# Padding four kinds of tiles to whole multiples of 128 bytes in a two-layer hybrid attention trunk

## The chip, the cores and the metric

One core of a Trainium2 chip runs the whole program, in one launch. The metric is the device time of an execution in microseconds, of which the median of several runs is taken; lower is better.

## The reference

Two layers over 256 tokens of width 1024, in float32. Each layer normalises x, multiplies it by one wide input matrix, runs four small attention branches (stick breaking, gated linear, gated delta rule, dilated) of four heads each on slices of the product, gates and merges them, projects the result, adds it to x, and then does the same with an MLP of width 4096 with a squared relu.

```python
def hybrid_layer(x, g_mix, g_mlp, w_in, ..., w_branch, w_out, w_mlp_in, w_mlp_out):
    h = rms_norm(x, g_mix)
    (sb_q, sb_k, sb_v, gla_q, ..., dil_v, gate_logits) = jnp.split(h @ w_in, IN_OFFSETS, axis=-1)
    o_sb = stick_breaking_attention(...)
    o_gla = gla_branch(...)
    o_dn = deltanet_branch(...)
    o_dil = dilated_branch(...)
    gates = jax.nn.sigmoid(gate_logits.reshape(B, S, N_BRANCH, D_MODEL))
    merged = jnp.zeros_like(x)
    for n, o in enumerate((o_sb, o_gla, o_dn, o_dil)):
        merged = merged + gates[:, :, n] * (o.reshape(B, S, BRANCH_WIDTH) @ w_branch[n])
    x = x + merged @ w_out
    h = rms_norm(x, g_mlp)
    return x + jnp.square(jax.nn.relu(h @ w_mlp_in)) @ w_mlp_out
```

## The kernel before

**The stream of weights.** All weights lie in HBM as a list of units of 128 x 2048 float32, in the order in which they are used. Half a unit (128 x 1024, 512 KB) is loaded at a time into a tile raw (six of them), and split into two parts of type float32r: whi by a cast on ACT (line 247), wlo as the rest on DVE (line 248), five buffers of each. Activations are split in the same way into a high and a low part. A product is then three passes of matmuls: high by high, high weights by low activations, low weights by high activations.

**The dense matmuls.** All go through the helper mm (line 198 and 199), mm(out, stationary, moving). Each loads 128 x 128 weights and moves 256 columns, 1024 bytes in each partition. Half a unit makes 24 of them.

- Input products, gates and the first MLP product (unit_F, mmF, line 398): weights whi or wlo stationary, activations ah or al (8 x 256 columns) moving, one PSUM bank with the tag bg at a time. Three of the input products go token by token (unit_T, line 417), with ah or al stationary and whi or wlo moving.
- Branch products (unit_br, line 1246): whi or wlo stationary, oh or ol moving, in banks bg.
- Output projection and second MLP product (units_out, line 447): whi or wlo stationary, and mh or ml (output projection) or uh or ul (MLP, 32 x 256 columns each) moving, summed over all units in four banks fa and fb, eight sums at once.
- The small product "mini" (unit_mini, line 431): whi stationary with 64 columns instead of 128, ah or al moving.

**The small work.** The four branches run as threads of generators that take one step after each half of a unit (small, line 1139), with matmuls of their own in float32 (line 199 too) and transposes against the identity at the beginning of the tile C.

**Where tiles lie.** Pools are laid out one behind another in each partition: cons (C, MK, x, PR, NR), wp (raw, whi, wlo), acts (ah, al), sm (small tiles, among them nea), and then the pool of a stage: for the mixing (d6 three times, mg, s8, dlT0, ..., oh, ol), for the MLP (uh, ul, rl, sq). Each tile takes its bytes rounded up to a multiple of 32. C begins at byte 16512, a multiple of 128, and takes 5696 bytes (1422 columns); PR takes 3488 (2 x 433 columns); nea takes 32, twice; d6 takes 6240 (6 x 260 columns), three times. All others from C to ah are multiples of 128. From these sizes follow the offsets modulo 128: raw, whi, wlo, ah, al and NR at 96, the MLP's uh and ul at 32, and in the mixing mh, ml, oh, ol and the tiles of the branches at 64, d6 at 32, 96 or 0. The steps inside a tile (1024 bytes between slices of activations, 512 or more between those of weights) are multiples of 128.

Of the kernel before, what the change touches and what calls it, by code (L numbers as in the profile page):

```python
# [9 lines left out]
F32 = mybir.dt.float32  # L10
# [9 lines left out]
NL = 2  # L20
# [53 lines left out]
# columns of the packed parameters of a layer  # L74
P_GMIX, P_GMLP, P_CONV, P_DTB, P_ALOG, P_GLAB = 0, 8, 16, 40, 44, 48
P_GLAG, P_DNG, P_DILQ, P_DILK, P_LR2, NPAR = 49, 113, 177, 241, 305, 433
# columns of the constants
C_ID, C_NEGU, C_NEG1, C_UT, C_GT, C_STR, C_SBN, C_DIL = 0, 128, 256, 384, 512, 640, 768, 896
C_COS, C_SIN, C_SEL, C_S32, C_I32, C_H4, C_AB, NCON = 1280, 1312, 1344, 1346, 1378, 1410, 1414, 1422
LV = (1, 2, 4, 8, 16, 32, 64)  # L80

# [37 lines left out]
def lay_out(inp):  # L119
    a = {k: np.asarray(v) for k, v in inp.items()}  # L120
    w_in, w_br, w_out, w_mi, w_mo = (a[k] for k in ("w_in", "w_branch", "w_out", "w_mlp_in", "w_mlp_out"))
    W = np.zeros((len(UNITS), 128, 2048), np.float32)

    def kcols(w, c0, n=256):
        """[p][kt][column]"""
        return w[:, c0:c0 + n].reshape(8, 128, n).transpose(1, 0, 2).reshape(128, 8 * n)

    def fcols(w, c0):
        """[p][half of the columns][kt][column]"""
        return w[:, c0:c0 + 256].reshape(8, 128, 2, 128).transpose(1, 2, 0, 3).reshape(128, 2048)  # L130

    def krows(w, r0, halves=1):
        """[p][half of the columns][kt][column]"""
        n = 1024 // halves
        return w[r0:r0 + 256].reshape(2, 128, halves, n).transpose(1, 2, 0, 3).reshape(128, 2048)

    for n, (l, kind, arg) in enumerate(UNITS):
        if kind == "inF":
            W[n] = fcols(w_in[l], OFF[arg])
        elif kind == "inT":  # L140
            W[n] = kcols(w_in[l], OFF[arg])
        elif kind == "mini":
            m = np.zeros((1024, 32), np.float32)
            m[:, 0:8] = w_in[l][:, 2320:2328]
            m[:, 8:24] = w_in[l][:, 1280:1296]
            W[n][:, :256] = kcols(m, 0, 32)
        elif kind == "gate":
            W[n] = fcols(w_in[l], OFF["gates"] + arg[0] * 1024 + arg[1] * 256)
        elif kind == "br":
            W[n] = krows(w_br[l, arg], 0, 2)  # L150
        elif kind == "wo":
            W[n] = krows(w_out[l], arg * 256)
        elif kind == "mi":
            W[n] = fcols(w_mi[l], arg * 256)
        else:
            W[n] = krows(w_mo[l], arg * 256)
    P = np.zeros((NL, 128, NPAR), np.float32)
    for l in range(NL):
        P[l][:, P_GMIX:P_GMIX + 8] = a["norm_mix_g"][l].reshape(8, 128).T
        P[l][:, P_GMLP:P_GMLP + 8] = a["norm_mlp_g"][l].reshape(8, 128).T  # L160
        P[l][:, P_CONV:P_CONV + 24] = a["dn_conv_w"][l].reshape(6, 128, 4).transpose(1, 0, 2).reshape(128, 24)
        P[l][:, P_DTB:P_DTB + 4] = a["dn_dt_bias"][l][None]
        P[l][:, P_ALOG:P_ALOG + 4] = a["dn_a_log"][l][None]
        P[l][:, P_GLAB] = a["gla_b_lr"][l]
        P[l][:, P_GLAG:P_GLAG + 64] = a["gla_norm_g"][l][None]
        P[l][:, P_DNG:P_DNG + 64] = a["dn_norm_g"][l][None]
        P[l][:, P_DILQ:P_DILQ + 64] = a["dil_q_norm_g"][l][None]
        P[l][:, P_DILK:P_DILK + 64] = a["dil_k_norm_g"][l][None]
        for r in (8, 40):
            P[l][r:r + 16, P_LR2:P_LR2 + 128] = a["gla_w_lr2"][l]  # L170
    X = np.ascontiguousarray(a["x"].reshape(256, 8, 128).transpose(2, 1, 0).reshape(128, 2048))
    C, M = constants()
    return {"xin": X, "w": W, "par": P, "con": C, "msk": M}


@with_exitstack
def trunk(ctx: ExitStack, tc: tile.TileContext, xin, w, par, con, msk, out, dbg=None, nl=NL):
# [14 lines left out]
    def r3(ap, a):  # L192
        return ap.rearrange("p (a b) -> p a b", a=a)
# [10 lines left out]
    # ---------------- constants and x  # L204
    C = cons.tile([128, NCON], F32, name="C")
    MK = cons.tile([128, 5 * 128], U8, name="MK")
    x = cons.tile([128, 8, 256], F32, name="x")
    PR = cons.tile([128, NL, NPAR], F32, name="PR")
# [18 lines left out]
    # ---------------- the stream of weights  # L227
# [22 lines left out]
    def split_upto(h):  # L250
        """h counts halves of units"""
        while state["split"] <= min(h, 2 * total - 1):
            k = state["split"]
            hi = wp.tile([128, 1024], F32R, name="whi", bufs=HALVES)
            lo = wp.tile([128, 1024], F32R, name="wlo", bufs=HALVES)
            splits[k] = (hi, lo)
            src = raws.pop(k)
            if wcols(k // 2) == 256:
                # both parts side by side
                src, both = r3(src[:, :128], 4), r3(hi[:, :256], 4)  # L260
                ACT.copy(both[:, :, 0:32], src)
                DVE.tensor_sub(both[:, :, 32:64], src, both[:, :, 0:32].bitcast(F32))
            elif k == 0:
                state["first"] = (src, hi, lo)
            else:
                n = 512 if k == 1 else 1024
                for c in range(0, 1024, n):
                    split_part(src, hi, lo, slice(c, c + n))
            state["split"] += 1
            dma_upto(k + RAW)  # L270
# [15 lines left out]
    nc.sync.dma_start(C[:, C_NEG1 + 128:], con[:, C_NEG1 + 128:])  # L286
# [4 lines left out]
    # ---------------- small helpers  # L291
    def rsqrt(v, n, name):
        """v: [128, n] in SBUF, > 0"""
        y = sm.tile([128, n], F32, name=name + "y")
        t = sm.tile([128, n], F32, name=name + "t")
        first_guess(v, y, t)
        yield from pause(name)
        newton(v, y, t, POOL if NPOOL else None)
        return y

    def pause(name):
        """slack between a step and the one that reads it on another engine, in halves of units"""
        for _ in range(PAUSE[name]):
            yield
# [19 lines left out]
    class Norm:  # L324
        """x times the gain, feature-major and split; the root mean square is applied to what is made of it"""
# [28 lines left out]
        def rows(self):  # L354
            """1 / rms of each token, on every partition"""
# [9 lines left out]
        def scaled(self, t):  # L365
            """x over the root mean square"""
            self.t = t
            for kt in range(8):
                POOL.tensor_tensor(t[:, kt, :], x[:, kt, :], self.R, op=OP.mult)  # L369

        def flip(self):
            """from here on what is made of it needs no scale"""
# [12 lines left out]
    def half(h, evac_first=False):  # L385
        """weights of half h of the current unit; the halves after it are begun"""
# [11 lines left out]
    def mmF(o, wh, wl, c, h, kts=8, new=False):  # L398
        """feature-major product: three passes; that over the operand split last comes last"""
# [8 lines left out]
    def unit_F(h, new=False):  # L408
        """yields after each half, then a bank [128, 2, 256], feature-major; new: h has only just been made"""
# [7 lines left out]
    def unit_T(h):  # L417
        """token-major, a bank [128, 2, 256]"""
# [12 lines left out]
    def unit_mini(h):  # L431
        """feature-major [64, 256]: by the high parts of the weights and, 32 rows on, by the low ones"""
# [14 lines left out]
    def units_out(h, units, nm):  # L447
        """feature-major products in four banks [128, 2, 256], added to x; the last unit goes by output"""
# [49 lines left out]
    # ---------------- one layer  # L498
# [31 lines left out]
    def mixing(l, pr, mp, nm):  # L530
# [7 lines left out]

        def split_pair(ps):
# [4 lines left out]
        def to_feature(o, br, tag):  # L544
            """o: token-major [128, 2, 256] in SBUF -> split feature-major"""
# [7 lines left out]
        def head_rms(o, gs, br, tag, need=None):  # L553
            """o: [128, 2, 4, 64]; gs: silu of the gate times the gain"""
# [16 lines left out]
        # ---- gated delta rule: the gates and their decays  # L571
        def decay_chain():
            yield ("mini",)
            nea = sm.tile([128, 4], F32, name="nea")
# [24 lines left out]
            # rows and columns of the running sums of g  # L599
# [15 lines left out]
            got["E"] = E = T([6, 260], "d6", 3).rearrange("p a b -> p (a b)")[:, :1536].rearrange(  # L615
# [11 lines left out]
        # the products with the queries, and the values  # L627
# [33 lines left out]
        # ---- gated delta rule  # L661
        def dn_chain():
# [4 lines left out]
            pre = T([6, 260], "d6", 3)[:, :, :256]  # L667
# [38 lines left out]
            MT = T([6, 260], "d6", 3).rearrange("p a b -> p (a b)")[:, :1536].rearrange(  # L706
# [23 lines left out]
            # (I + M)^-1 transposed: blocks of 32 by substitution, all heads at once, then by doubling.  # L730
            # mc[j, (t, h), k]: the blocks of -M transposed
# [31 lines left out]
            def half_y(t, s):  # L763
                """levels 32 and 64: only the blocks below the diagonal"""
# [69 lines left out]
        # ---- stick breaking  # L834
# [54 lines left out]
        # ---- dilated  # L889
        def rope_chain():  # L890
            yield ("dil_q", "dil_k")
            qk = got["dil_qk"]                                  # [128, 16 (q/k, t, h), 64]
# [94 lines left out]
        # ---- gated linear attention  # L987
# [41 lines left out]
        def gla_chain():  # L1029
# [24 lines left out]
            # the diagonal and the pairs of level 1, a column of each for a head  # L1054
# [14 lines left out]
            # levels 16 to 2, two at a time; two heads at a time  # L1069
# [31 lines left out]
        # ---- threads of small work beside the weights  # L1101
        done = set()

        class Thread:
# [4 lines left out]
            def advance(self):  # L1109
                """one stage; False when it must wait or is over"""  # L1110
# [53 lines left out]
        cin = T([6, 260], "d6", 3)[:, :, :259]  # L1164
# [129 lines left out]
    with tc.tile_pool(name="boot", bufs=2) as bp:  # L1294
        # the tensor engine is brought to its full clock while the first loads are under way
# [42 lines left out]
```

## Time and profile before

| | |
|---|---|
| time, median of 3 runs | 932.86 us (930.16 to 934.34) |
| span of the profiled execution | 932.1 us |
| mean granted clock of TensorE | 0.983 |
| PE busy | 910.4 us, 7678 matmuls |
| DVE, ACT, POOL busy | 630.8, 534.4, 143.8 us |
| moved from HBM | 147.5 MB, 159 GB/s over the span |

The profile gives no time of its execution beside the span; the span and the median are 0.8 us apart. PE is TensorE's matmuls, PEld its weight loads, which run beside them. Matmuls overlap: one that takes 280 ns from start to end begins 113 to 120 ns after the one ahead of it. So a line's mean duration doesn't tell the pace; the distance between starts does. The timeline merges like instructions that follow closely into one line with a count; its first number is the start of the first of them.

### The profile page before, as it was taken

To read this page: it belongs to the slowest core of one execution; us is meant where nothing else is said; L and a number is where in the kernel's file an instruction comes from. 1 tells how busy PE (TensorE), PEld (TensorE's weight loads), DVE (VectorE), ACT (ScalarE), POOL (GpSimd) and SP (SyncE) were. 2 spreads that over 40 slices of the span, in tenths; PEclk is the share of its full clock that TensorE was granted. 3 is DMA by queue.
4 is the path that set the end of the run, shared out by engine and by line. 5 is a ranking of instruction groups with operands and counts; after the bars stand their busy time and mean duration, and the time that the engine had idled before them with its cause. 6 is when DMAs were issued, how large, how long until landed. Compare 5 with 4: busy or idle time off the path is not lost.

```text
span 932.1 us, 18924 instructions
## 1 busy us (share of the span) xinstructions
PE 910.4 (98%) x7678; PEld 884.4 (95%) x7678; DVE 630.8 (68%) x1242; ACT 534.4 (57%) x842; POOL 143.8 (15%) x148
## 2 busy tenths in 40 slices
PE   8999999999999999999989999999999999999998
PEld 6899999999998999999988999999999989999998
DVE  5959999429577676644489599984485867665442
ACT  5596758754554655543456876586545545654331
POOL 3524201113212000000042450013030120000000
PEclk7999999999999999999999999999999999999999
DMA  8544454433544556656444445444344535656551
GB/s 278 199 139 133 140 178 135 144 130 114 162 142 171 174 190 201 203 188 197 152 135 142 142 132 168 158 138 153 98 154 135 208 113 183 204 197 198 191 161 46
DMA packets 43430, 149.78 MB, mean 161 GB/s; under 512 B 4944, under 2 KB 7248, under 8 KB 43344
## 3 DMA queue, kind: packets, MB, share of 16 engines
q1 hardware_dynamic: 43056, 148.35, 48.8%
q8 instruction: 60, 0.98, 0.4%
q10 hardware_dynamic: 288, 0.23, 0.1%
q14 instruction: 26, 0.21, 0.1%
HBM read 147.51 MB, written 1.05 MB: 159 GB/s over the span
## 4 chain that ended last, share of the span: by engine, by line
PE 84%; DVE 8%; ACT 3%; POOL 2%; issue 1%; DMA 1%; SPq 0%; DVEq 0%; ACTq 0%
PE bg L199 55%; PE fa L199 14%; PE fb L199 14%; POOL s L369 2%; DVE al L339 2%; DVE wlo L248 2%; ACT whi L247 1%; DVE x L486 1%; DMA x<-xin 1%; POOL sbs L859 1%; DVE s L1082 0%; DVE ush L751 0%; DVE ush L749 0%; DVE s L1068 0%; PE fb L972 0%
## 5 line engine op out<-in xcount | busy, mean ns | idle before, releaser
L248 DVE TENSOR_TENSOR wlo<-raw,whi 128x1024 fp32r<-128x1024 f32 (+2 forms) x280 | 350.0, 1268 | 183.0 <-ACT whi L247 182.9
L247 ACT CAST whi<-raw 128x1024 fp32r<-128x1024 f32 (+2 forms) x280 | 283.8, 1034 | 117.9 <-PE bg L199 58.2
L199 PE MATMUL bg<-ah,whi 128*128 128x256 f32 x1232 | 315.2, 292 | 6.4 <-ACT ah L375 4.6
L199 PE MATMUL bg<-al,whi 128*128 128x256 f32 x1232 | 305.6, 289 | 6.2 <-DVE al L339 6.2
L199 PEld LDWEIGHTS bg<-ah,whi 128*128 128x128 f32 x1232 | 239.6, 194 | 13.3 <-ACT ah L375 6.6
L199 PEld LDWEIGHTS bg<-al,whi 128*128 128x128 f32 x1232 | 238.7, 196 | 7.6 <-DVE al L339 7.4
L199 PE MATMUL bg<-ah,wlo 128*128 128x256 f32 x1216 | 179.6, 286 | 1.5 <-DVE wlo L248 1.5
L199 PEld LDWEIGHTS bg<-ah,wlo 128*128 128x128 f32 x1216 | 162.5, 195 | 2.5 <-DVE wlo L248 2.5
L199 PE MATMUL fa<-uh,whi 128*128 128x256 f32 x256 | 70.4, 276 | 0.0
L199 PE MATMUL fa<-uh,wlo 128*128 128x256 f32 x256 | 70.4, 276 | 0.0
L199 PE MATMUL fa<-ul,whi 128*128 128x256 f32 x256 | 69.7, 276 | 0.0
L199 PE MATMUL fb<-uh,whi 128*128 128x256 f32 x224 | 61.6, 276 | 0.0
L199 PE MATMUL fb<-uh,wlo 128*128 128x256 f32 x224 | 61.6, 276 | 0.0
L199 PE MATMUL fb<-ul,whi 128*128 128x256 f32 x224 | 61.0, 276 | 0.0
L513 ACT ACTIVATE sq<-rl 128x512 f32<-128x512 f32 x32 | 20.2, 632 | 70.3 <-DVE rl L512 70.3
L445 DVE TENSOR_TENSOR ul<-sq,uh 128x512 fp32r<-128x512 f32 x32 | 22.2, 693 | 43.2 <-ACT uh L444 43.2
L1271 POOL TENSOR_TENSOR mg<-mg,gt 128x512 f32<-128x512 f32 x20 | 31.1, 1572 | 129.2 <-DVE gt L1270 129.2
L199 PEld LDWEIGHTS fa<-uh,whi 128*128 128x128 f32 x256 | 48.1, 188 | 0.0
L199 PEld LDWEIGHTS fa<-uh,wlo 128*128 128x128 f32 x256 | 48.1, 188 | 0.0
L199 PEld LDWEIGHTS fa<-ul,whi 128*128 128x128 f32 x256 | 47.6, 188 | 0.0
L199 PEld LDWEIGHTS fb<-uh,whi 128*128 128x128 f32 x224 | 42.1, 188 | 0.0
L199 PEld LDWEIGHTS fb<-uh,wlo 128*128 128x128 f32 x224 | 42.0, 188 | 0.0
(276 smaller groups left out, 1470.5 us busy)
## 6 DMA issues: line engine op xcount, KB each, us to landing
raw<-w SPq DMA_DIRECT2D x275, 512.0 KB, 4.3
x<-xin SPq DMA_DIRECT2D x3, 256.0 KB, 6.1
out_dram<-x SPq DMA_DIRECT2D x3, 256.0 KB, 2.1
C<-con SPq DMA_DIRECT2D x1, 519.0 KB, 6.9
raw<-w SPq DMA_DIRECT2D x4, 128.0 KB, 5.3
gt<-msk SPq DMA_DIRECT2D x2, 160.0 KB, 4.7
x<-xin SPq DMA_DIRECT2D x2, 128.0 KB, 2.8
raw<-w SPq DMA_DIRECT2D x4, 64.0 KB, 3.9
```

The costliest lines, as they stand in the source:

```text
L199: PE.matmul(o, l, r, start=start, stop=stop, skip_group_check=True)
L247: ACT.copy(hi[:, c], src[:, c])
L248: DVE.tensor_sub(lo[:, c], src[:, c], hi[:, c].bitcast(F32))
L339: DVE.scalar_tensor_tensor(self.h[1][:, kt, :], x[:, kt, :], self.g[:, kt:kt + 1], self.h[0][:, kt, :].bitcast(F32), op0=OP.mult, op1=OP.s ...
L369: POOL.tensor_tensor(t[:, kt, :], x[:, kt, :], self.R, op=OP.mult)
L445: DVE.tensor_sub(lo, src, hi.bitcast(F32))
L486: DVE.tensor_add(xs, pairs[fp], xs)
L513: ACT.activation(sq, rl, AF.Square)
L859: POOL.tensor_tensor(sp[:, :, c:c + 128], sp[:, :, c:c + 128], over(STR, 2), op=OP.mult)
L1271: (DVE if n == GLA and MADD[fp] else POOL).tensor_tensor(m, m, g, op=OP.add)
```

## The change

Four kinds of tiles get columns that nothing uses, so that each takes a multiple of 128 bytes, or (nea) brings the sum of its pool to one: C 1422 to 1440 columns (5760 bytes), PR 866 to 896 (3584 bytes), each d6 1560 to 1568 (6272 bytes), each nea 4 to 16 (64 bytes). What is read and written in them stays the same, by slices and rearrangements of the larger tile. Everything that lies behind them moves: weights, activations, uh, ul, oh, ol, mh, ml and the tiles of the branches all begin at a multiple of 128 then. The rest of the diff takes out comments.

```diff
+def whole(n):
+
+    return -(-n // 32) * 32
...
-    C = cons.tile([128, NCON], F32, name="C")
+    C = cons.tile([128, whole(NCON)], F32, name="C")
...
-    PR = cons.tile([128, NL, NPAR], F32, name="PR")
+    PR = cons.tile([128, whole(NL * NPAR)], F32, name="PR")[:, :NL * NPAR].rearrange("p (l c) -> p l c", l=NL)
...
-    nc.sync.dma_start(C[:, C_NEG1 + 128:], con[:, C_NEG1 + 128:])
+    nc.sync.dma_start(C[:, C_NEG1 + 128:NCON], con[:, C_NEG1 + 128:])
...
+        def d6():
+            return T([whole(6 * 260)], "d6", 3)
...
-            nea = sm.tile([128, 4], F32, name="nea")
+            nea = sm.tile([128, 16], F32, name="nea")[:, 0:4]
...
-            got["E"] = E = T([6, 260], "d6", 3).rearrange("p a b -> p (a b)")[:, :1536].rearrange(
+            got["E"] = E = d6()[:, :1536].rearrange(
                 "p (a h c) -> p a h c", a=3, h=4)
...
-            pre = T([6, 260], "d6", 3)[:, :, :256]
+            pre = r3(d6()[:, :1560], 6)[:, :, :256]
...
-            MT = T([6, 260], "d6", 3).rearrange("p a b -> p (a b)")[:, :1536].rearrange(
+            MT = d6()[:, :1536].rearrange(
                 "p (a h c) -> p a h c", a=3, h=4)
...
-        cin = T([6, 260], "d6", 3)[:, :, :259]
+        cin = r3(d6()[:, :1560], 6)[:, :, :259]
```

## Rows read from the trace of the kernel before

**Rows 1.** Page, part 1: busy us, share of the span, instructions.

```profile
PE 910.4 (98%) x7678; PEld 884.4 (95%) x7678; DVE 630.8 (68%) x1242; ACT 534.4 (57%) x842; POOL 143.8 (15%) x148
```

**Rows 2.** Page, part 4: chain that ended last, by engine, by line.

```profile
PE 84%; DVE 8%; ACT 3%; POOL 2%; issue 1%; DMA 1%; SPq 0%; DVEq 0%; ACTq 0%
PE bg L199 55%; PE fa L199 14%; PE fb L199 14%; POOL s L369 2%; DVE al L339 2%; DVE wlo L248 2%; ACT whi L247 1%; DVE x L486 1%; DMA x<-xin 1%; POOL sbs L859 1%; DVE s L1082 0%; DVE ush L751 0%; DVE ush L749 0%; DVE s L1068 0%; PE fb L972 0%
```

**Rows 3.** Waits of PE: line, releaser, us in total, times, longest us.

```profile
PE bg L199 <- DVE al L339: 6.2, 6, 1.0
...
PE bg L199 <- ACT whi L247: 1.8, 3, 1.4
PE bg L199 <- DVE wlo L248: 1.5, 2, 1.1
...
PE fa L549 <- DVE Y L566: 0.9, 2, 0.6
```

**Rows 4.** Windows of three stages: PE, PEld, DVE, ACT, POOL busy (count), clock, DMA, GB/s.

```profile
300.00:380.00 80.00, 80.00 (x669) 80.00 (x668) 53.99 (x61) 46.92 (x61) 0.00 (x0) 1.00 0.57 185
384.00:468.00 84.00, 84.00 (x743) 84.00 (x742) 39.83 (x35) 34.03 (x35) 0.00 (x0) 1.00 0.58 186
265.00:285.00 20.00, 20.00 (x172) 20.00 (x171) 16.81 (x20) 11.35 (x16) 1.68 (x1) 1.00 0.63 221
```

**Rows 5.** Timeline of PE, first MLP product: start us, us, instruction, count.

```profile
329.96 1.12 PE L199 MATMUL bg<-ah,wlo 128*128 128x256 f32 x8
330.92 0.28 PE L199 MATMUL bg<-ah,whi 128*128 128x256 f32 x1
```

**Rows 6.** Timeline of PE, second MLP product; five more starts lie between.

```profile
400.01 0.28 PE L199 MATMUL fa<-uh,wlo 128*128 128x256 f32 x1
...
400.69 0.28 PE L199 MATMUL fb<-uh,wlo 128*128 128x256 f32 x1
```

**Rows 7.** Window of PE at the lower clock: busy, count, clock, DMA, GB/s.

```profile
292.80:295.80 3.00, 3.00 (x16) 0.50 0.52 162
```

**Rows 8.** Timeline of weight loads: two-column matmuls, then transposes.

```profile
58.86 1.31 PEld L199 LDWEIGHTS fa<-C,Y 128*128 128x128 f32 x11
...
115.05 0.91 PEld L928 LDWEIGHTS fb<-C,dil_qk 128*128 128x128 f32 x8
```

**Rows 9.** Timeline of PE, sums of the stick-breaking branch (512, 256, 256 columns, twice).

```profile
75.79 1.10 PE L199 MATMUL fb<-sp,NR 128*128 128x512 f32 x6
76.73 0.28 PE L199 MATMUL bg<-whi,ah 128*128 128x256 f32 x1
```

**Rows 10.** Groups of PE by form: count, busy us, mean ns, idle before.

```profile
L199 PE MATMUL bg<-ah,whi 128*128 128x256 f32 x1216 | 311.5, 292 | 6.4 <-ACT ah L375 4.6 <-ACT whi L247 1.8
...
L199 PE MATMUL fa<-uh,whi 128*128 128x256 f32 x256 | 70.4, 276 | 0.0
...
L199 PE MATMUL bg<-oh,whi 128*128 128x256 f32 x128 | 35.3, 296 | 1.1 <-DVE gt L1270 1.1
...
L199 PE MATMUL bg<-whi,ah 128*128 128x256 f32 x224 | 32.7, 288 | 0.0
...
L199 PE MATMUL fa<-mh,whi 128*128 128x256 f32 x64 | 17.8, 282 | 0.0
```

**Rows 11.** Cores: span and mean granted clock.

```profile
core 0: 932.1 us, clock 0.983
```

**Rows 12.** Groups of DVE and ACT that split the weights.

```profile
L248 DVE TENSOR_TENSOR wlo<-raw,whi 128x1024 fp32r<-128x1024 f32 x274 | 345.9, 1280 | 177.4 <-ACT whi L247 177.3
...
L247 ACT CAST whi<-raw 128x1024 fp32r<-128x1024 f32 x274 | 281.1, 1047 | 117.9 <-PE bg L199 58.2 <-PE fb L199 55.9 <-issue 2.8
```

**Rows 13.** Timeline of PE, the product with 64 weight columns; nine more starts between.

```profile
26.86 0.28 PE L199 MATMUL bg<-ah,whi 128*64 128x256 f32 x1
...
28.00 0.28 PE L199 MATMUL bg<-ah,whi 128*64 128x256 f32 x1
```

## Prediction

> **What bounds the kernel now.** I read the engines' shares first: PE is busy for 910 of 932.1 us, DVE for 631 [rows 1]. Then the chain that ended last: 84% of it is PE, nearly all at line 199, the one matmul helper [rows 2]. Then PE's own list of waits: its eight entries, from 6.2 us for the split activations down to 0.9, come to under 20 us [rows 3]. So what counts is how far apart PE starts its matmuls. The "mean ns" of a group (276 to 292) is no help, since matmuls overlap; I take the distance of starts, from a stretch without a gap (its length over its count, less two that reach in from outside) or from the starts in the order of time.
>
> That distance is not the same everywhere, though nearly every dense matmul has the same shape, 128x128 weights and 256 moving columns. In the first MLP product it is 80 us / 667 = 119.9 ns, in the second 84 / 741 = 113.4 ns, in the output projection of the mixing 20 / 170 = 118 ns, all at a granted clock of 1.00 [rows 4]. Single starts say the same: eight in 0.96 us with ah [rows 5], six in 0.68 us with uh and ul [rows 6]. What differs is where the operands lie. By the tile sizes, modulo 128 bytes: weights whi and wlo at 96 always; ah and al at 96 too; mh, ml, oh and ol at 64; uh and ul at 32. So, as (moving, stationary): (96, 96) costs 119.9, (64, 96) 118, (32, 96) 113.4 ns. [...]
>
> **The change, part by part.** No instruction, wait, queue or order changes. C grows by 64 bytes as laid out, PR by 96, the two nea by 32 each, each of the three d6 by 32; everything behind them moves, and all dense operands land on offset 0. The pair (0, 0) is nowhere in the trace, so its distance c is the unknown, and it has to be bounded.
>
> From below: 107 ns, half of the row at the lower level [rows 7]. Nearer by: the loading of 128 weight columns has a pace of its own. Matmuls of only 2 moving columns, which have next to nothing to stream, still load 0.112 us apart (11 loads in 1.31 us, the last taking 0.19), and transposes of 128 columns, whose moving operand is the identity at offset 0 of C, load 0.110 us apart (8 in 0.91, the last 0.14) [rows 8]. From above: 119.9, the worst pair there is.
>
> I take 112. The three pairs stand in an order: a run that begins 32 bytes behind a multiple of 128 costs 113.4, one at 64 costs 118, one at 96 costs 119.9; offset 0 continues this on the good side, and what then remains is the pace of the weight loads, 110 to 112. A second row speaks for the beginning of the run itself: the stick-breaking group of six streams 2048 columns in eight runs of 256 from offset 64, in 0.94 us or 117.5 ns a run [rows 9]; two of its matmuls have two runs on one weight load, so half as much loading per run, and the runs still cost as much as in the output projection.
>
> How many: 1216 x 3 matmuls with ah or al, 224 x 3 token-major, 128 x 3 with oh or ol, 64 x 6 with mh or ml, 512 x 3 with uh or ul (one group of each kind in [rows 10]; fa, fb and bg share the 512 of uh with whi as 256, 224 and 32). About 5% of all but the last stand at the lower level or behind a wait, where c doesn't count (an estimate: a mean granted clock of 0.983 [rows 11] is 3.4% of the time at the lower level, and the waits are 2%).
>
> - (3648 + 672) x 0.95 = 4104, each from 119.9 to 112: 32.4 us
> - (384 + 384) x 0.95 = 730, each from 118 to 112: 4.4 us
> - 1536, each from 113.4 to 112: 2.1 us
>
> Sum: 38.9 us. Against it I put 2 us. Half a unit is 24 matmuls, 2.88 us now and 2.69 then, and beside it the casts (1047 ns), the low parts (1280 ns) and a 512 KB load must fit [rows 12]. ACT and DVE fit (in the first MLP product DVE is busy 54 of 80 us, and would be 54 of 75); the DMA moves 185 GB/s there [rows 4] and would move 198. But the small chains of the mixing step forward with PE's halves, and a few of their waits in [rows 3] will be longer by what PE gains. The waits there end on ACT and DVE chains and don't shrink.
>
> The other addresses move as well. Casts and low parts at shifted offsets are off the path: PE waited 1.8 and 1.5 us in all for them [rows 3], so I put nothing; a tenth more on each would still fit under 2.69 us, and a tenth less would free nobody. The loads of raw begin at 0 instead of 96 and are six halves ahead; nothing. Of the small matmuls those of 2 columns run at the load's pace with weights at offset 64 already [rows 8], so I put nothing for them all, with 1 us either way.
>
> The span is 932.1 us and the median 932.9, so next to nothing lies around the span and I work from the median: 932.9 - 38.9 + 2 = 896.0.
>
> [...] Rows first: with the same shape the distance is 113.4 at one pair of offsets and 119.9 at another [rows 4]. [...] Second, loads of 64 weight columns instead of 128, with the same moving tile at 96 and weights at 96, start 114 ns apart (ten in 1.14 us) against 119.9 [rows 13]: what the weight load reads does slow the stream. [...]
>
> **The rivals.**
>
> - *The distance between the two reads, not the beginning.* Modulo 128 the pairs differ by 0 (119.9), 32 (118) and 64 (113.4): the price falls with the distance between the operands as well as with the offset of the moving one, and this trace cannot part the two, as all dense weights sit at 96. If two streams that begin at the same offset collide wherever they begin, (0, 0) is another (96, 96). Then ah and al gain nothing, oh, ol, mh and ml lose 1.9 ns (730 x 1.9 = 1.4 us), and the second MLP product, fast by luck today, loses 6.5 ns: 1536 x 6.5 = 10.0 us. 932.9 + 11.4 = 944. For it: the half-size loads [rows 13] show that the load matters. Against it: those same rows have distance 0 and cost 114, and the runs of [rows 9]. It decides from c = 118.1 on, where the gains of the 4104 (1.8 ns each) and the losses of the 1536 (4.7 ns) cancel.
> - *Both.* The beginning costs some 4 ns and the distance the rest: c around 116.5. 4104 x 3.4 + 730 x 1.5 - 1536 x 3.1 = 10.3 us less: 923.
> - *Neither.* The stages differ in something other than offsets (the second MLP product keeps eight sums open in four banks, the first one bank at a time), and aligning changes nothing: 933. Against it: the output projection has the same loops as the second MLP product, and stands at 118 [rows 4].
>
> **How the numbers follow.** Forecast, c from 109 to 113.4: 62%; at 109 the sum is 4104 x 10.9 + 730 x 9 + 1536 x 4.4 = 58 us (877), at 113.4 it is 30 us (905). Both: 12%. Neither: 6%. Distance: 20%. The range that leaves out no more than 2 in 10 takes in all but the last, from 876 to 934; the forecast's own is 876 to 905. Half a percent, about what a measurement can tell from no change, is 4.7 us: faster 74%, within it 6%, slower 20%.
>
> **What would show it.** In the profile after, eight starts of the first MLP product should take about 0.90 us instead of 0.96, and the stretches of both MLP products should have the same distance, near 112. If both stand at 119.9 the distance rival holds; if the second MLP product keeps 113.4 and the first joins it, c is 113.4 and the gain is 30 us. DVE and ACT sums should not move. PE's waits should stay under 22 us; if they grow by 10 or more, the cover of the halves is gone and the step with the 2 us is wrong. At the lower level the distance should stay at 214 ns.

## The result and the profile after

The changed kernel takes 942.39 us (median; 940.36 to 947.24) against 932.68 us for the kernel before in the same session: ratio 1.0118, 95% interval 1.0085 to 1.0152. It is slower by 1.2%; 896 us was predicted, in a range that ended at 934.

First the page of the changed kernel: the span, the engines (busy us, share, instructions), the chain by engine, and one group of matmuls of the second MLP product (busy us, mean ns, idle before). Lines have moved: the matmul helper, line 199 before, is line 204.

```profile
span 938.6 us, 18924 instructions
PE 917.6 (98%) x7678; PEld 891.6 (95%) x7678; DVE 630.4 (67%) x1242; ACT 534.0 (57%) x842; POOL 143.1 (15%) x148
PE 85%; DVE 8%; POOL 2%; ACT 2%; issue 1%; DMA 1%; SPq 0%; DVEq 0%
L204 PE MATMUL fa<-uh,whi 128*128 128x256 f32 x256 | 72.2, 283 | 0.0
```

Set beside [rows 1, 2]: the same instructions, the same chain, DVE and ACT within 0.4 us. PE alone is busy longer, by 7.2 us. The windows of the two MLP products (PE, PEld, DVE, ACT, POOL busy and count, clock, DMA, GB/s) say where:

```profile
300.00:380.00 80.00, 80.00 (x669) 80.00 (x668) 54.61 (x62) 46.94 (x60) 0.00 (x0) 1.00 0.58 188
384.00:468.00 84.00, 84.00 (x702) 84.00 (x701) 37.35 (x31) 31.30 (x31) 0.00 (x0) 1.00 0.55 176
```

Against [rows 4] the first MLP product has not moved: 669 matmuls, 80 us / 667 = 119.9 ns. The second has lost 41 of its 743: 84 / 700 = 120.0 ns where it was 113.4. The timelines of single starts answer [rows 5, 6]: start, length, instruction. The first pair of lines stands eight starts apart (seven lie between), the second pair six, the third, of the output projection, ten.

```profile
330.01 0.28 PE L204 MATMUL bg<-ah,whi 128*128 128x256 f32 x1
...
330.97 0.28 PE L204 MATMUL bg<-ah,whi 128*128 128x256 f32 x1
```

```profile
400.09 0.28 PE L204 MATMUL fa<-uh,wlo 128*128 128x256 f32 x1
...
400.81 0.28 PE L204 MATMUL fb<-uh,wlo 128*128 128x256 f32 x1
```

```profile
285.02 0.28 PE L204 MATMUL fb<-ml,whi 128*128 128x256 f32 x1
...
286.21 0.28 PE L204 MATMUL fb<-mh,wlo 128*128 128x256 f32 x1
```

Eight starts with ah still take 0.96 us; six with uh and ul take 0.72 instead of 0.68; the output projection stands at 119 ns.

Joined with the byte at which each operand begins (the addresses of the compiled program), the starts of the whole trace at the upper clock level (granted clock 1.00) add up like this: the 1535 intervals of uh and ul rose from 174.0 to 184.2 us, so by 10.2 us; ah and al stayed at 119.8 and 119.9 ns, the token-major ones at 119.8, oh, ol, mh and ml went from 118.3 to 118.7. The profiled span grew by 6.5 us only (932.1 to 938.6), because that execution had 209 dense starts at the lower level (granted clock 0.50, as in [rows 7]) or just around it, where the profiled one of before had 245; the medians differ by 9.7.

So the loss has one address: the second MLP product.

### The profile page after: what moved, and what is told of

It reads as the page before. It is cut to its first block, busy times and chain, and to the rows that moved or that the text cites. A ratio compares the mean times of both kernels' runs of the same rounds, so it can differ in the third digit from the quotient of the medians.

```text
span 938.6 us, 18924 instructions
## 1 busy us (share of the span) xinstructions
PE 917.6 (98%) x7678; PEld 891.6 (95%) x7678; DVE 630.4 (67%) x1242; ACT 534.0 (57%) x842; POOL 143.1 (15%) x148
## 4 chain that ended last, share of the span: by engine, by line
PE 85%; DVE 8%; POOL 2%; ACT 2%; issue 1%; DMA 1%; SPq 0%; DVEq 0%
PE bg L204 54%; PE fa L204 15%; PE fb L204 14%; POOL s L374 2%; DVE al L344 2%; DVE wlo L253 2%; ACT whi L252 1%; DVE x L491 1%; DMA x<-xin 1%; POOL sbs L867 1%; DVE s L1090 0%; DVE ush L759 0%; DVE ush L757 0%; DVE s L1076 0%; PE fb L980 0%
## 5 line engine op out<-in xcount | busy, mean ns | idle before, releaser
L253 DVE TENSOR_TENSOR wlo<-raw,whi 128x1024 fp32r<-128x1024 f32 (+2 forms) x280 | 346.3, 1255 | 191.5 <-ACT whi L252 191.4
L204 PE MATMUL bg<-al,whi 128*128 128x256 f32 x1232 | 302.3, 287 | 6.2 <-DVE al L344 6.2
L518 ACT ACTIVATE sq<-rl 128x512 f32<-128x512 f32 x32 | 20.2, 632 | 70.3 <-DVE rl L517 70.3
```

Of the source, the lines that this page charges most:

```text
L204: PE.matmul(o, l, r, start=start, stop=stop, skip_group_check=True)
L253: DVE.tensor_sub(lo[:, c], src[:, c], hi[:, c].bitcast(F32))
L518: ACT.activation(sq, rl, AF.Square)
```

## The experiments

Two theories were to be told apart. *Beginning*: the price goes by the byte where the moving operand begins. *Distance*: it goes by how far the moving operand begins behind the weights, wherever the two lie. Distances are given modulo 256 bytes; why 256 and not 128 is shown further down. A spacing is the mean time from one dense start to the next at the upper clock level.

**One pad out, one pad in.** Only the pads of the two nea, which move what lies behind them by 64 bytes, decide whether uh and ul land at distance 0. Leaving it out of the changed kernel puts them 192 behind the weights, as they were before, but at another byte; putting it alone into the kernel before puts them at distance 0 and aligns nothing (weights at 96 modulo 128).

```diff
 # e1_no_nea: the changed kernel with
-nea = sm.tile([128, 16], F32, name="nea")[:, 0:4]
+nea = sm.tile([128, 4], F32, name="nea")
 # e2_nea_only: the kernel before with
-nea = sm.tile([128, 4], F32, name="nea")
+nea = sm.tile([128, 16], F32, name="nea")[:, 0:4]
```

> The changed kernel without the columns added to nea: weights and ah, al stay at offset 0, but uh, ul, oh, ol, mh, ml come to lie at 64 modulo 128. Distance theory (what counts is how far apart, modulo 128, the moving operand and the weights begin): the second MLP product is at distance 64 again, as in the kernel before, and starts 113.4 ns apart; ah and al stay at distance 0 and 119.9; total about 932 to 933. Theory of the moving operand's own offset (64 cost 118 in the kernel before, whatever the weights): the second MLP product stands at 118, total about 940. Theory that weights at 0 are the cause: 120, total 942.

> The kernel before with the columns added to nea alone: weights, ah and al stay at 96; uh and ul move from 32 to 96, so nothing of the dense MLP work is aligned to 128. Distance theory: uh and ul are at distance 0 and start 120 ns apart, total about 942 to 944, the whole loss of the change with none of its alignment. Theory that offset 0 itself is bad (a start at a multiple of 128 costs 120): uh and ul at 96 are not at 0; by the row of ah at 96 they could still be at 120, so this run parts the theories only together with e1.

Without the pad: 932.38 us, ratio to the kernel before 1.0004 (0.9982 to 1.0025). With the pad alone: 943.11 us, ratio 1.0122 (1.0079 to 1.0164). The second MLP product in windows of PE alone (busy, count, clock, DMA, GB/s), first without the pad, then with the pad alone:

```profile
390.00:465.00 75.00, 75.00 (x664) 1.00 0.57 182
```

```profile
390.00:465.00 75.00, 75.00 (x628) 1.00 0.57 182
```

75 / 662 = 113.3 ns at distance 192, 75 / 626 = 119.8 ns at distance 0, whether the weights are at 0 or at 96. That falsifies *beginning* for this product, which had 118 for the 64 of e1_no_nea, and gives the whole of the change's loss to these two pads. What is still aligned in e1_no_nea (the weights, and ah and al together with them) was worth nothing that can be measured: 1.0004. The tiles oh to ml aren't aligned there: they begin 64 behind the weights and start 117.7 ns apart.

**What at distance 0 costs the time.** Half the weight load, everything else as in the changed kernel: the second MLP product loads only 64 of each 128 weight columns, so half of what it adds to x is left out, and half the rows are written.

```diff
 # e8_half_load: the changed kernel, in units_out
+M = 64 if units == 16 else 128
 ...
-wh, wl = (q[:, ft * 128:ft * 128 + 128] for q in wt)
+wh, wl = (q[:, ft * 128:ft * 128 + M] for q in wt)
 ...
```

> The changed kernel, in which the second MLP product loads and computes only the first 64 of every 128 output columns (half of what it adds to x is left out); the moving operands, their number and all offsets stay, distance 0. If the moving reads are held up by the weight load beside them: 113 to 114 ns instead of 120, about 10 us less than the changed kernel, 932. If the moving operand alone is slow at distance 0 or offset 0: 120 and 942.

One run: 935.72 us, at a mean granted clock of 0.979 (0.987 in the profile of the changed kernel), where 932 was expected. Window of PE in the second MLP product:

```profile
390.00:465.00 75.00, 75.00 (x664) 1.00 0.59 186
```

113.3 ns (1019 intervals of 113, 509 of 114) where the same moving operand at the same byte costs 120.0 beside a whole load. So the moving read alone costs no more than 113.3 at that byte; the other 6.7 ns go with the second half of the load or of the written rows, which this edit halves together. That it is the load is argued, not shown: in e1_no_nea the output is the same as in the changed kernel, and the distance to the weights alone takes the same 6.7 ns away.

**The price of each distance.** The changed kernel with ah, al and uh, ul each taken at a chosen byte of a tile that is 256 bytes longer, another for each stage, so that one run measures up to six distances.

```diff
 # e3, e4, e6, e7, e10, e11: the changed kernel, lists differ
+ACT_AT, U_AT = [32, 64, 96, 160], [64, 128]
 ...
 def new_act():
-    return (acts.tile([128, 8, 256], F32R, name="ah"), acts.tile([128, 8, 256], F32R, name="al"))
+    o = ACT_AT[state["norm"]] // 4
+    state["norm"] += 1
+    return tuple(r3(acts.tile([128, 2048 + 64], F32R, name=n)[:, o:o + 2048], 8) for n in ("ah", "al"))
 ...
-uh = mp.tile([128, 32, 256], F32R, name="uh")
-ul = mp.tile([128, 32, 256], F32R, name="ul")
+o = U_AT[l] // 4
+uh, ul = (r3(mp.tile([128, 8192 + 64], F32R, name=n)[:, o:o + 8192], 32) for n in ("uh", "ul"))
```

> The changed kernel with the activations shifted inside larger tiles, another shift for each stage: ah and al begin 32, 64, 96 and 160 bytes behind a multiple of 128 (first mixing, first MLP, second mixing, second MLP), uh and ul 64 in the first layer and 128 in the second; weights at 0 throughout. Distance theory: 64 gives 113.4 ns in both kinds of product; 32, 96 and 160 give 116 to 119; 128 gives 120. Theory of the moving operand's own offset, by the rows of before: 32 gives 113.4, 64 gives 118, 96 gives 119.9.

> The same with other shifts: ah and al at 192, 224, 128 and 16 bytes in the four stages, uh and ul at 48 in the first layer and 16 in the second; weights at 0. Distance theory modulo 128: 192 is as 64 (113.4), 224 is as 96 (116 to 119), 128 is as 0 (120), 16 lies between 0 and 32, 48 between 32 and 64 (114 to 117). If the period is 256 and not 128, 192 and 64 differ. Theory of the moving operand's own offset: 192 as 64, 118; 128 as 0, 120.

> The changed kernel with shifts inside larger tiles: ah and al begin 80, 192, 112 and 72 bytes behind the weights modulo 256 (first mixing, first MLP, second mixing, second MLP), uh and ul 208 in the first layer and 200 in the second. One speed for each distance: 192 gives 113.4 in the first MLP product too; 72 and 200, near 64 and 192, tell how narrow the good distance is: within 1 ns of 113.4 or 117.8 if the price changes slowly, 118 or more if it is narrow. Two patterns: the first MLP product of the first layer has stretches at 113.4 and at 117.8.

> The same with ah and al at 56, 184, 240 and 176 bytes and uh and ul at 4 in the first layer and 188 in the second. Distance theory: 4 is nearly 0, 119 to 120; 184 and 188 are near 192, 113.4 if the good distance is broad; 240 is as 112 modulo 128, 118 to 120; 176 as 48, 118.

> The changed kernel with ah and al at 104, 112, 120 and 240 bytes in the four stages (first mixing, first MLP, second mixing, second MLP) and uh and ul at 112 in the first layer and 240 in the second. Period 128: 240 is as 112, 113.4 to 114.5 in the long stretches of the second MLP as in the first. Period 256: 240 stands at 117, as in the scan before. 104 and 120, no multiples of 16: 116 to 121, as 56, 72, 184 and 200 were.

> The same with ah and al at 116, 108, 100 and 124 bytes and uh and ul at 120 in the first layer and 104 in the second. If only multiples of 16 are good: all between 118 and 123. If the good distance is broad around 112: 108 and 116 at 113.4 to 115.

Spacing by distance, from these runs and from the kernels above, the token-major matmuls left out (ns; where two operands had the same distance, both; "or" parts two paces of one kernel):

| distance | ns | distance | ns | distance | ns |
|---|---|---|---|---|---|
| 0 | 119.8, 120.0 | 96 | 119.9 | 160 | 118.6 |
| 4 | 123.3 | 100 | 120.6 | 176 | 119.3 |
| 16 | 118.5, 118.7 | 104 | 120.0 or 127.5 (mean 123.5), 120.0 | 184 | 120.0 |
| 32 | 116.9, 117.5 | 108 | 120.0 | 188 | 119.7 |
| 48 | 118.3 | **112** | **113.3 to 114.4** | **192** | **113.4 or 117.8** |
| 56 | 119.9 | 116 | 121.6 | 200 | 120.0 |
| 64 | 117.8, rarely 113.4 | 120 | 121.0, 121.1 | 208 | 119.2 |
| 72 | 120.6 | 124 | 118.3 | 224 | 118.3 |
| 80 | 119.0 | 128 | 118.7, 119.0 | 240 | 117.2 |

The runs took 932.08, 934.59, 936.24, 939.75, 929.62 and 946.23 us in the order of the texts above (one run each, mixed distances, so the totals say little). Windows of PE in the first MLP product: distance 64 (e3_scan), 112 (e10_scan) and 108 (e11_scan).

```profile
305.00:375.00 70.00, 70.00 (x596) 1.00 0.60 198
```

```profile
305.00:375.00 70.00, 70.00 (x620) 1.00 0.58 193
```

```profile
305.00:375.00 70.00, 70.00 (x586) 1.00 0.59 194
```

70 / 594 = 117.8, 70 / 618 = 113.3, 70 / 584 = 119.9 ns. Three readings. Four bytes beside 112 the gain is gone. 112 and 240 differ by 128 and cost 113.3 and 117.2, so the period is not 128; it may be 256 or more. And alignment by itself earns nothing: 0 and 128, the two distances that the change can make, cost 120 and 118.7, and of the multiples of 16 in the table only 112 and 192 come down to 113.4 for a whole product. The multiples of 16 run from 113.3 to 120.0, and the distances that aren't multiples of 16 stand at 118.3 or more.

A distance doesn't always have one price. In e10_scan the first mixing, at 104, has stretches at 120.0 and others at 127.5, where starts are 122 and 138 ns apart by turns; in e11_scan uh and ul keep 120.0 at 104. A window of the slow kind (8 / 62 = 129 ns, edges counted):

```profile
157.00:165.00 8.00, 8.00 (x64) 1.00 0.61 197
```

At 64 one stretch of e1_no_nea (22 intervals of oh and ol) runs at 113.4, all others at 117.8. The token-major matmuls, in which activations and weights change places, agree with the table at 16, 128 and 224 and not at 160 and 200 (117.4 against 118.6, 117.9 against 120.0). And the expectations by distance missed twice: 64 was to cost 113.4, and 4 was to cost 119 to 120.

**All at 192.** The distance that was good for uh before, given to every dense operand that can have it; the same edit with ACT_AT = [192] * 4, U_AT = [128, 128] and 24 columns for nea.

> The changed kernel with every dense moving operand (ah, al, uh, ul, oh, ol, mh, ml) shifted to begin 192 bytes behind the weights, modulo 256; weights stay at multiples of 128. Distance theory with one speed for each distance: all feature-major products start 113.4 ns apart, the token-major ones (distance 64) about 117; against the kernel before 3650 x 6.5 + 648 x 2.8 + 727 x 4.9 = 29 us less, about 904. If a distance of 64 modulo 128 has two patterns, 113.4 and 117.8, and a stretch keeps the one it falls into (first seen in the short stretches of the first mixing with shift 192): some stretches at 117.8, total 905 to 925. Theory that alignment is what counts: 64 is off alignment, 940 or more.

926.8 us (7 runs, 920.53 to 931.38), ratio 0.9939 (0.9905 to 0.9973): a gain, but short of the 905 to 925 expected and about a quarter of the 22 us that 113.4 for ah and al alone would give (3427 intervals by 6.4 ns). Two windows with ah and al in an early stage, two of the output projection (first layer, then second), then the second MLP product, all of this kernel and all at distance 192:

```profile
92.00:99.00 7.00, 7.00 (x65) 1.00 0.46 150
102.00:109.00 7.00, 7.00 (x62) 1.00 0.42 140
269.00:281.00 12.00, 12.00 (x108) 1.00 0.94 320
727.00:739.00 12.00, 12.00 (x104) 1.00 0.90 317
390.00:465.00 75.00, 75.00 (x639) 1.00 0.55 175
```

7 / 63 = 111 and 7 / 60 = 117 ns in the short ones, whose edges count; by single intervals the first is all 113 and 114, the second all 117 to 119. The output projection stands at 12 / 106 = 113.2 in the first layer and 12 / 102 = 117.6 in the second, though the program lays out mh and ml alike in both layers. The long one is 75 / 637 = 117.7 ns. So distance 192 has two patterns, and a stretch keeps the one it begins with: the first MLP product holds 117.8 through 695 intervals and the second through the 768 behind it, without a change. In e1_no_nea the second MLP product ran at 113.4 with its operands at the same bytes modulo 256 (moving at 64, weights at 128). There it followed a product at 120, here one at 117.8. That the pattern is handed on is a guess. A rival for this pair of runs was not tested: by the sizes of the tiles uh begins 256 further here modulo 512, and ul does not. It can't account for the output projection, whose two windows differ in no tile size; what sets the pattern was not settled.

**All at 112, and 112 for the first MLP product's operands alone.** The scan's edit with ACT_AT = [112] * 4, U_AT = [48, 48] and 24 columns for nea (e9_dist112); and the kernel before, nothing aligned, with ah and al moved by 28 columns (e12_before112):

```diff
 # e12_before112: the kernel before with
-return (acts.tile([128, 8, 256], F32R, name="ah"), acts.tile([128, 8, 256], F32R, name="al"))
+return tuple(r3(acts.tile([128, 2048 + 64], F32R, name=n)[:, 28:28 + 2048], 8) for n in ("ah", "al"))
```

> The changed kernel with ah, al, uh and ul 112 bytes behind the weights modulo 256, and oh, ol, mh, ml 192 behind. In the scan the second mixing at 112 stood at 114.3 ns on the mean, most of it at 113.4. If that holds in the long stretches too: both MLP products at 113.4 to 114.5 and the mixing's feature-major products at 114.5, token-major at 120: 3650 x 5.3 + 727 x 3 = 21 to 22 us less than the kernel before, 909 to 912. If 112 is only as good as 192 with its two patterns (116.5 and 117.8): 921 to 930. If alignment to 16 or 32 bytes matters for itself (112 is a multiple of 16, not of 32): above 933.

> The kernel before with one edit: ah and al begin 112 bytes further on inside larger tiles; the weights stay at 96 modulo 128, uh and ul at 32, oh, ol, mh and ml at 64, so nothing is aligned and ah and al are at distance 112 modulo 256. If only the distance counts: feature-major products at 114.2 ns on the mean, as with the weights at 0, the second MLP product at 113.4; 3410 x 5.6 = 19 us of pace gained, less some 8 us of waits and stretches at the lower clock as in the run before: 918 to 922. If the good distance needs weights at a multiple of 128: ah and al at 116 to 120, 925 to 933.

All at 112 (oh to ml fall at 192 by it, at 113.5 to 115.5 ns): 918.7 us, ratio 0.9836 (0.9795 to 0.9878), where 909 to 912 was expected. The pace came as expected (ah and al at 114.2), but in its profile PE waits 3.8 us longer in all than before, and 53 more dense starts stand at or around the lower level, some 4 to 5 us. The kernel before with ah and al alone moved: **912.25 us** (911.59 to 913.55), ratio **0.9783** (0.9759 to 0.9808). It beats both kernels, with weights at 96 modulo 128 and no dense operand at a multiple of 128. Its page (engines), two windows of PE in the MLP products, and the first waits of PE (releaser: us in total, times, longest):

```profile
PE 886.2 (97%) x7678; PEld 859.9 (95%) x7678; DVE 630.0 (69%) x1242; ACT 534.7 (59%) x842; POOL 143.2 (16%) x148
```

```profile
305.00:375.00 70.00, 70.00 (x620) 1.00 0.60 197
390.00:455.00 65.00, 65.00 (x576) 1.00 0.56 181
```

```profile
PE bg L199 <- DVE al L339: 6.2, 6, 1.0
PE bg L199 <- ACT ah L375: 4.2, 9, 1.2
PE bg L199 <- ACT whi L247: 2.2, 3, 1.1
PE bg L199 <- DVE ol L445: 2.2, 2, 1.1
PE fa L549 <- DVE Y L566: 1.6, 2, 1.0
```

Both products stand at 113.3 (70 / 618, 65 / 574). Over the trace, 3469 intervals of ah and al went from 119.8 to 114.0: 20.1 us, which is the gain of the medians (20.2). In this run ah and al take 8448 bytes each, so they lie 256 apart modulo 512, and both start at 113.3 to 113.4 ns in the first MLP product: at 112 nothing asks for a period longer than 256. The time came out 6 us better than the expectation's lower end; this profile has 208 dense starts at or around the lower level where before had 245 and e9_dist112 298 (43, 52 and 62 us). Which execution has how many was not steered by any edit here, so this part is an observation.

## Why the prediction was wrong, point by point

**What bounds the kernel: right.** Only the spacing of PE's starts moved, and the time moved with it, in both directions (942.4 and 912.3 us) at the same instructions and the same DVE and ACT sums.

**The choice of c = 112: the step that failed.** The pair (0, 0) costs 119.9 to 120.0. The bounds were right, and c landed on the upper one. "Offset 0 continues this on the good side" drew a line through three pairs [rows 4] that differ in offset *and* in distance, as all weights lie at 96; a trace in which two causes move together can't be asked for the third point. Read by distance the same three are 0, 224 and 192, and (0, 0) isn't a new point but the first one again. The term of 4104 x 7.9 ns (32.4 us) was therefore nought, the 730 x 6 ns (4.4 us) came out at minus 0.4 ns each, and the 1536 x 1.4 ns (2.1 us) became a loss of 6.6 ns each. The lower bound of 107 ns was an estimate: half of 3 us / 14 = 214 ns at a granted clock of 0.50 [rows 7]. No run shows the 109 ns at which the forecast's range began; the lowest spacing of any distance was 113.3.

**The two rows that held me to it.** [rows 13], half-size loads at distance 0 for 114 ns, were put against the distance rival. They belonged to it: e8_half_load shows the same in the second MLP product, 113.3 instead of 120.0 at distance 0 with half the load. The eight runs of the stick-breaking group [rows 9] were read as a price of the run's beginning. The changed kernel has them at a multiple of 128, and there they take 0.94 us as before, so leaving 64 saved them nothing; why they cost 117.5 stays open. The rows that answer [rows 9]:

```profile
74.68 1.10 PE L204 MATMUL fb<-sp,NR 128*128 128x512 f32 x6
75.62 0.28 PE L204 MATMUL bg<-whi,ah 128*128 128x256 f32 x1
```

**The rival "distance": right in kind and nearly in size.** It gave 944 us; 942.4 was measured. Its large term, 1536 x 6.5 = 10.0 us, measured 10.2. Its small one was mis-sized: it had oh to ml at 119.9, as at distance 0, and they are at 118.7, 0.4 ns above before instead of 1.9, because they land 128 away from the weights and 128 is another distance than 0. The alignment of the change was to 128, and what counts repeats no sooner than 256; the rival had it modulo 128, by which 64 would be as good as 192, and 64 costs 117.8 in e3_scan. It had 20%, and the range was drawn to leave it out; with three confounded pairs and [rows 13] in hand it deserved about as much as the forecast, and the range should have reached 944.

**"Both" and "neither": fallen.** Where the change and e1_no_nea, e2_nea_only and e12_before112 put the operands, distance accounts for the spacings to about 1 ns; it does not for the two patterns at 192 and at 104. "Neither" fell with the output projection as the prediction said, and with e1_no_nea and e2_nea_only, where one pad moves the same loops from 113.3 to 120.

**The 2 us of lost cover: not tested by the change, about right in e12_before112.** There PE did gain 20 us, and its waits show what came late: ol with 2.2 us and Y with 1.6 instead of 0.9, against wlo with 0.4 instead of 1.5. That is 2 us, in the small chains of the mixing as said, and the casts and low parts still fit.

**The checks.** Eight starts of the first MLP product: 0.96 us, as for the distance rival. Both products at 119.9 to 120: "the distance rival holds". DVE and ACT sums unmoved: right. PE's waits: the eight longest entries are 17 us in all, so the cover held. The lower level: 215 ns on the mean, as before; what the distance costs at the upper level doesn't show there: 214 ns at distance 0 in [rows 7], and a mean of 214 to 216 in e9_dist112 and e12_before112, where ah and al are at 112. A window at that level in the changed kernel (busy, count, clock, DMA, GB/s):

```profile
496.30:498.90 2.60, 2.60 (x14) 0.50 0.00 0
```

14 less the two that reach in give 2.6 / 12 = 217 ns, with no transfer running.

## What to carry to other kernels

Where PE's dense matmuls stand more than a nanosecond or two above their best spacing in the same trace, list where both operands of each begin, and look at their distance, not at the alignment of either. No run here gives a rule that foretells the good distances, and one shape alone was measured (256 columns, float32r). A pad of a few bytes is then the cheapest experiment there is; here 64 bytes cost 1.2% and 112 bytes earned 2.2%. And where all evidence for a rule shares one value of another variable, as all weights here lay at 96, give the rival that uses that variable as much chance as the rule.

## What the runs showed of the hardware that was not expected

- The spacing of 256-column f32r matmuls with 128-column loads depends on the distance between the operands' beginnings: 113.3 ns at 112, 120.0 at 0, 121 to 123 at 4, 116 and 120. Halving the load at distance 0, and with it the written rows, brings it to 113.3.
- Distance 192 has two patterns, 113.4 and 117.8 ns, and a stretch keeps its own for hundreds of starts (695 and 768 in e5_dist192). Its output projection, laid out alike in both layers, stands at 113.2 in a window of the first and at 117.6 in one of the second. Distance 104 has stretches at 120.0 and at 127.5 in e10_scan.
- No distance came below 113.3 ns; at the lower level the mean of the starts is 214 to 216 ns in the kernels before and after and in e1, e2, e9 and e12 alike.
- Open: why 112 is good and 240 is not, what chooses the pattern at 192 and at 104, and whether there is a period longer than 256 anywhere but at 112.
